# Later conditioning on TensorE behind the first tiles, query and key splits after their transposes, folded weights in plain float32

## The chip, the cores and the metric

The kernel runs on one core of one Trainium2 chip. The metric is device time in microseconds (us) for one launch. Five engines work side by side: TensorE (PE; its weight loads, PEld, overlap with it), VectorE (DVE), ScalarE (ACT), GpSimd (POOL) and SyncE (SP), whose queue issues the DMAs.

## The reference, cut to what matters

One step of a two-layer backbone on 1024 latent and 256 context tokens with 1024 channels. Both layers are modulated by a conditioning vector: `c` for latent tokens, `c_ctx` for context tokens.

```python
def ada_mod(cvec, w, b):
    m = jax.nn.silu(cvec) @ w + b              # (1024) @ (1024, 3072): shift, scale, gate
    return jnp.split(m, 3, axis=-1)

# each layer: h = rms_norm(x, g) * (1 + scale) + shift;  x = x + gate * mixer(h)
# layer 0: two attention mixers (A global, B windowed +-128 with a sink logit), 8 query and
#   2 key/value heads of 64 each; A's q and k are RMS-normed per head; rotary positions on
#   latent q and k; latent tokens also attend to cached context keys and values;
#   y = concat(oa * silu(ga), ob * silu(gb)) @ w_out
# layer 1: u, gate = split(h @ w_in, 2);  y = (Re(fft2(u in 4 groups of 256)) * silu(gate)) @ w_out
# at the end: rms_norm(x, final_g)
```

Outputs are the two token streams and the new context keys and values of layer 0.

## The kernel before, in words

**Precision.** Most matmuls are split: each operand is held as a high part (float32r, a rounded float32) and a low part (the rest), and `mm3` (L236) adds three products, hi x hi, hi x lo and lo x hi. `split` (L259) makes the parts, one cast and one subtraction. A matmul on tiles of type float32 that were not split runs in plain float32; the first layer's conditioning does so already.

**Buffers.** `take(tag, ...)` gives a buffer of a zone (`u` 26, `w` 8, `q` 2, `pt` 3, `p` 4, `h` 9, `e` 4), the one that has been free longest among the zones named; `drop` gives it back. PSUM has eight banks in four tags; transposes go through the three banks of `t`.

**Order of the work.** The program is written out flat, and the framework's planner orders each engine's queue, SP's too, by a simulated timeline of its own with program order as priority. Attention and its fillers are ordered by hand: `attend` (L968) runs over units (128-query tile, group g, head pair pr; groups 0 and 1 are mixer A, 2 and 3 mixer B). A unit is `soft` (scores, row minima, exponential), then `weigh` of an earlier unit (transposes of the probabilities, split, product with the values), then `fl_.pump(budget)`, which lets queued filler work run up to a budget in us.

The stages:

1. *Start.* Group 0's folded weights (`fold_load` L506, `fold_piece` L526: layer 1's input weights times the channel Fourier matrix, written to DRAM as `wcd`, `wsd`), the loads of x, and for each of 8 channel chunks the layer-0 shift and scale on TensorE (`ada_load` L468, `ada_chunk` L477: two tiles of 8 x 128 x 128 weights, 16 plain matmuls of the 2-column conditioning with 128 columns of weights, then two small transposes), modulation, and the first key and query products of tiles 0 to 3.
2. *First tiles* (`S1`, L31, loop at L799): norm and modulation of the other token groups, then keys and values (`kv_pair` L673) and queries (`q_pair` L723) of mixer A. Each of these evacuates a product, norms and rotates it, splits it (`split_v` L627, hi in 64 columns and lo in the next 64), and leaves a `post` for later: transposes of the split halves (`transp` L631, 128 columns a head) and their copy out of PSUM. Keys stay in SBUF for mixer A or go to DRAM (`kd`) for B; queries go to DRAM (`qd`) and are loaded by `load_q` (L830) when a unit needs them. `fl_.depth` posts are held back.
3. *Attention A and B*, with fillers in the order of `ORDER` (L50): query weights, mixer B's keys, folded weights f1, gates g0 to g3, folded weights f2, f3. In qb0, qb1 and g0 stands the later conditioning, `COND` (L51): the gate of layer 0 and the shift and scale of layer 1. `cond_steps` (L1017) calls `Rows.step_ap` (L340) for each of 8 rows of weights (4 KB a partition): two products added up on VectorE for the latent vector (L345), a scaled copy on ScalarE (L349) and an addition on GpSimd (L350) for the context vector. `Rows.finish` (L369) splits the accumulators and sums them over partitions with 8 matmuls of 512 columns (L359), then writes the gate to DRAM (`gtd`) or transposes shift and scale into columns (`row_to_mod` L300).
4. *Turn to the output projection.* `weigh` stores each unit's output to DRAM (`od`, through `store` L929) at once; when all units of a row tile are finished, `proj_load` and `proj_step` (L1207, L1216) load it back with gates and softmax totals and multiply by `w_out` (tile name `oz`). Output weights come through `out_weights` (L983).
5. *Layer 1*: gates (`g1E`, `g1O`, `g1c`), Fourier products (`u`, `pc`, `ps`), output projection (`of`).

Of the kernel before, what the change touches and what calls it, by code (L numbers as in the profile page):

```python
# [9 lines left out]
F32 = mybir.dt.float32  # L10
# [7 lines left out]
P = 128  # L18
D = 1024
NT = 10  # L20
# [13 lines left out]
EF = 1  # L34
PLACE = (
# [9 lines left out]
FC, XF = 1.3, False  # L45
AT_C, WO1 = (1, 1), ((0, 1, 2, 3), (), (4,), (5, 6), (7,))
# [4 lines left out]
COND = ("qb0", "qb1", "g0")  # L51
# [70 lines left out]
def hybrid_step(ctx: ExitStack, tc: tile.TileContext, I, O):  # L122
# [44 lines left out]
    qd = dr.tile([NT, 4, 2, 64, 512], F32, name="qd")  # L167
# [26 lines left out]
    bT1 = cp.tile([P, 8], F32, name="bT1")  # L194
# [121 lines left out]
    class Rows:  # L316
# [23 lines left out]
        def step_ap(self, k):  # L340
            wt = take(self.tags, (P, D))
            sp.dma_start(wt.a, ada_src(self.l, self.part, k))
            for h in range(2):
                sl = slice(h * 512, h * 512 + 512)
                dve.scalar_tensor_tensor(  # L345
                    out=self.acc[0][:, sl], in0=wt[:, sl], scalar=cs[:, k, 0:1], in1=self.acc[0][:, sl],
                    op0=ALU.mult, op1=ALU.add,
                )
            act.activation(wt.a, wt.a, AF.Copy, scale=cs[:, k, 1:2])  # L349
            pool.tensor_add(self.acc[1].a, self.acc[1].a, wt.a)  # L350
            drop(wt)

# [114 lines left out]

    def ada_load(k):  # L468
        out = []
        for part in range(2):  # L470
            raw = take(("p", "pt", "q"), (P, 8, P))
            c0 = part * D + k * P
            sp.dma_start(raw.a, I["ada_w"][0, :, c0 : c0 + P].rearrange("(b p) c -> p b c", p=P))
            out.append(raw)
        return out

    def ada_chunk(k, raws):  # L477
        ps = bank("g", f"ada{k}")
        for part, raw in enumerate(raws):
            for b in range(8):  # L480
                pe.matmul(
                    ps[0:2, part * P : part * P + P], cs[:, b, :], raw[:, b, :], start=b == 0, stop=b == 7
                )
            drop(raw)
# [7 lines left out]
        dve.tensor_scalar(moda[:, 0, k, :], tp[:, 2:4], bT1[:, k : k + 1], gT[:, 0, k : k + 1], op0=ALU.add, op1=ALU.mult)  # L492
# [13 lines left out]
    def fold_load(g):  # L506
        if "f" not in fold:
            fraw = take("h", (P, 2, 256))
            sp.dma_start(fraw.a, I["fch"])
            fold["f"] = (take("h", (P, 2, 256), F32R), take("h", (P, 2, 256), F32R))  # L510
            split(fold["f"][0].a, fold["f"][1].a, fraw.a)
            drop(fraw)
        wu = []
        for j in range(2):
            hi = take("w", (P, 1024), F32R)
            lo = take("w", (P, 1024), F32R)
            for hf in range(2):
                raw = take("h", (P, 512))
                sl = slice(hf * 512, hf * 512 + 512)
                sp.dma_start(raw.a, I["wuT"][(2 * g + j) * P : (2 * g + j + 1) * P, sl])  # L520
                split(hi[:, sl], lo[:, sl], raw.a, XE["wh"], E_WL)
                drop(raw)
            wu.append((hi, lo))
        return wu

    def fold_piece(g, kb2, wu, tag="g", later=None):  # L526
        fh, fl = fold["f"]
        acc = bank(tag, f"wa{g}{kb2}")
        for i in range(2):
            c0 = (2 * kb2 + i) * P  # L530
            mm3(
                acc[:, i * 256 : i * 256 + 256],
                [(wu[j][0][:, c0 : c0 + P], wu[j][1][:, c0 : c0 + P], fh[:, j, :], fl[:, j, :]) for j in range(2)],
            )
# [13 lines left out]
        if kb2 == 3:  # L548
            for h, l in wu:
                drop(h, l)  # L550
            fold["n"] = fold.get("n", 0) + 1
            if fold["n"] in (EF, 4):
                drop(fh, fl)
# [14 lines left out]
    dve.tensor_scalar(bT1, bT[:, 0, 8:16], 1.0, None, op0=ALU.add)  # L568
# [62 lines left out]
    def transp(name, y2, n):  # L631
        tp = t_bank(name, F32R)
# [1184 lines left out]
```

## Time and profile before

| | |
|---|---|
| median of 3 runs | 1280.24 us (1274.92 to 1284.47) |
| profiled execution, its own time | 1273.2 us |
| its span | 1271.3 us |
| DMA moved in all | 168.28 MB, 132 GB/s on average |
| mean granted TensorE clock | 0.979 |

In the profile `out<-in` names the tiles an instruction writes and reads, with buffer numbers left out (`h`, `w`, `u` and so on are the zones). Matmuls and weight loads are both listed with their line; a line can be that of a helper such as L243 in `mm3`. Durations of single matmuls include the pipeline's depth, so that a row of n matmuls takes less than n times the mean. The chain of waits follows the work that ended last back from the end: at each step to what released it.

### The profile page before, as it was taken

To read this page: it belongs to the slowest core of one execution; us is meant where nothing else is said; L and a number is where in the kernel's file an instruction comes from. 1 tells how busy PE (TensorE), PEld (TensorE's weight loads), DVE (VectorE), ACT (ScalarE), POOL (GpSimd) and SP (SyncE) were. 2 spreads that over 40 slices of the span, in tenths; PEclk is the share of its full clock that TensorE was granted. 3 is DMA by queue.
4 is the path that set the end of the run, shared out by engine and by line. 5 is a ranking of instruction groups with operands and counts; after the bars stand their busy time and mean duration, and the time that the engine had idled before them with its cause. 6 is when DMAs were issued, how large, how long until landed. Compare 5 with 4: busy or idle time off the path is not lost.

```text
span 1271.3 us, 21928 instructions
## 1 busy us (share of the span) xinstructions
PE 1194.0 (94%) x7867; PEld 1061.1 (83%) x7867; DVE 928.8 (73%) x2105; ACT 625.9 (49%) x1223; POOL 458.7 (36%) x376
## 2 busy tenths in 40 slices
PE   7979999999899899999999979789999998999997
PEld 6769999999789888888999978667777888988886
DVE  4478888776987987868887868466775888558553
ACT  4343466665575576755756676431264324333121
POOL 4256665423785764530101042310411216335001
PEclk9989999999999999999999989889999999999999
DMA  9902322324634345444332398597412544345321
GB/s 306 291 5 66 92 91 57 115 72 120 179 101 137 96 139 176 120 129 128 90 107 80 93 264 205 154 254 199 134 42 76 163 152 142 101 156 177 132 85 66
DMA packets 156198, 168.28 MB, mean 132 GB/s; under 512 B 21917, under 2 KB 117161, under 8 KB 156090
## 3 DMA queue, kind: packets, MB, share of 16 engines
q1 hardware_dynamic: 156090, 166.89, 44.6%
q8 instruction: 62, 1.02, 0.4%
q14 instruction: 46, 0.38, 0.1%
HBM read 122.67 MB, written 44.18 MB: 131 GB/s over the span
## 4 chain that ended last, share of the span: by engine, by line
PE 69%; DVE 12%; DMA 9%; issue 4%; POOL 3%; ACT 2%; SPq 1%; POOLq 0%; DVEq 0%; ACTq 0%
PE of L243 9%; PE ga L243 8%; PE av L951 7%; PE pt L945 6%; PE oz L243 5%; PE q L243 4%; PE u L243 4%; PE g1E L243 4%; PE g1O L243 3%; PE sL L828 3%; PE kv L243 2%; DVE w L345 2%; PE sC L828 2%; PE g1c L243 2%; DVE p L862 2%
## 5 line engine op out<-in xcount | busy, mean ns | idle before, releaser
L948 DVE TENSOR_TENSOR pt<-pt,pt 128x512 fp32r<-128x512 f32 (+1 forms) x264 | 170.9, 657 | 32.2 <-ACT pt L255 31.9
L951 PE MATMUL av<-pt,u 128*128 128x256 f32 x1008 | 171.3, 292 | 7.8 <-DVE pt L948 4.5
L255 ACT ACTIVATE pt<-pt 128x512 fp32r<-128x512 f32 (+1 forms) x264 | 146.9, 574 | 60.9 <-PE pt L945 35.6
L945 PE MATMUL pt<-identr,p 128*128 128x128 f32 x1008 | 156.6, 274 | 0.8 <-ACT h L255 0.5
L951 PEld LDWEIGHTS av<-pt,u 128*128 128x128 f32 x1008 | 142.1, 192 | 17.1 <-DVE pt L948 7.8
L261 POOL TENSOR_TENSOR w<-h,w 128x512 fp32r<-128x512 f32 x58 | 76.8, 1337 | 184.6 <-ACT w L255 79.0
L243 PE MATMUL q<-w,u 128*128 128x256 f32 x864 | 130.4, 291 | 0.7 <-ACT h L731 0.7
L945 PEld LDWEIGHTS pt<-identr,p 128*128 128x128 f32 x1008 | 119.6, 141 | 9.9 <-DVE pt L948 1.0
L243 PE MATMUL ga<-u,w 128*128 128x512 f32 (+1 forms) x576 | 123.6, 360 | 0.1
L869 ACT ACTIVATE p<-p,nm 128x1280 f32<-128x1280 f32 (+1 forms) x80 | 95.4, 1192 | 54.5 <-DVE p L862 54.0
L243 PEld LDWEIGHTS q<-w,u 128*128 128x128 f32 x864 | 115.7, 193 | 4.3 <-ACT h L731 1.2
L243 PEld LDWEIGHTS ga<-u,w 128*128 128x128 f32 x576 | 93.8, 188 | 15.0 <-ACT pt L255 0.6
L828 PE MATMUL sL<-u,q 128*128 128x512 f32 x256 | 85.0, 417 | 10.4 <-DVE p L862 8.3
L243 PE MATMUL oz<-u,w 128*128 128x512 f32 x240 | 69.2, 416 | 11.2 <-ACT w L255 11.2
L869 ACT ACTIVATE p<-p,NM 128x640 f32<-128x640 f32 (+2 forms) x80 | 59.2, 740 | 32.8 <-DVE p L862 32.7
L350 POOL TENSOR_TENSOR w<-w,w 128x1024 f32<-128x1024 f32 x24 | 58.4, 2433 | 44.6 <-ACT w L349 33.7
L828 PE MATMUL sC<-u,q 128*128 128x256 f32 x320 | 63.4, 301 | 9.0 <-DMA q<-qd 5.2
L243 PE MATMUL of<-u,u 128*128 128x512 f32 (+1 forms) x219 | 66.0, 389 | 0.0
L243 PEld LDWEIGHTS oz<-u,w 128*128 128x128 f32 x240 | 46.6, 200 | 21.6 <-ACT w L255 11.9
L828 PEld LDWEIGHTS sC<-u,q 128*128 128x128 f32 x320 | 49.1, 193 | 13.1 <-DMA q<-qd 5.8
L862 DVE TENSOR_SCALAR_CACHE_REDUCE p<-sC,nsink 128x256 f32<-128x256 f32 x80 | 37.8, 475 | 30.2 <-PE sC L828 25.2
L345 DVE SCALAR_TENSOR_TENSOR w<-w,cs,w 128x512 f32<-128x512 f32 x48 | 52.7, 1136 | 5.3 <-DMA w<-i_ada_w 4.2
(771 smaller groups left out, 2802.8 us busy)
## 6 DMA issues: line engine op xcount, KB each, us to landing
q<-qd SPq DMA_DIRECT2D x80, 256.0 KB
w<-i_ada_w SPq DMA_DIRECT2D x24, 512.0 KB
h<-i_w_in SPq DMA_DIRECT2D x40, 256.0 KB
qd<-h SPq DMA_DIRECT2D x40, 256.0 KB
h<-i_w_out SPq DMA_DIRECT2D x32, 256.0 KB
h<-i_wuT SPq DMA_DIRECT2D x16, 256.0 KB
u<-i_x SPq DMA_DIRECT2D x8, 512.0 KB
p<-i_ada_w SPq DMA_DIRECT2D x8, 512.0 KB
```

The costliest lines, as they stand in the source:

```text
L243: pe.matmul(out, a, b, start=i == 0, stop=i == n - 1)
L255: act.activation(out, in_, AF.Copy)
L261: pick("lo" + lc, lc).tensor_sub(dst_l, src, dst_h)
L345: dve.scalar_tensor_tensor(out=self.acc[0][:, sl], in0=wt[:, sl], scalar=cs[:, k, 0:1], in1=self.acc[0][:, sl], op0=ALU.mult, op1=ALU.add,)
L350: pool.tensor_add(self.acc[1].a, self.acc[1].a, wt.a)
L828: pe.matmul(ps, q[:, s, hc * P : hc * P + P], keys, start=s == 0, stop=s == 1)
L862: dve.tensor_scalar(p[i][:, end[i] : end[i] + n], ps, sign, last[i], op0=ALU.mult, op1=ALU.min, accum_out=c)
L869: act.activation(p[i][:, 0 : end[i]], p[i][:, 0 : end[i]], AF.Exp, bias=last[i], scale=-1.0, accum_out=SU[:, t, hd + i, 0:1],)
L945: pe.transpose(tp[:, jj * 256 + i * P : jj * 256 + i * P + P], p[i][:, off : off + P], ident)
L948: dve.tensor_sub(pt[:, 1, 0:n], tp[:, 0:n], pt[:, 0, 0:n])
L951: pe.matmul(acc, vv, pt[:, s, jj * 256 : jj * 256 + 256], start=c + jj + s == 0, stop=c + jj == nt - 1 and s == 1,)
```

## The change

- *Later conditioning.* `step_ap`, `cond_steps` and `COND` go. Instead 24 column tiles (gate of layer 0, shift and scale of layer 1, 8 each) are loaded as the first layer's are (512 bytes a row), multiplied on TensorE by the 2-column conditioning (8 plain float32 matmuls each) and placed between the steps of the first tiles: `AT_N` says how many before each step. A gate tile gets its bias and goes to DRAM; a shift or scale tile is copied out, transposed (one tile later) and modulated.
- *Splits after transposes.* `kv_pair` and `q_pair` transpose the unsplit float32 result, two heads in 128 columns, so half as many transposes, and make hi and lo out of PSUM: one copy and one subtraction (`key_split`, `post`). `qd` and `kd` have another layout; `load_q`, `scores` and `swap_kv` follow it. Cached keys are treated the same way, with both heads' columns loaded.
- *Folded weights.* `fold_load` keeps the weights and the Fourier matrix unsplit, `fold_piece` multiplies them in plain float32.
- *Order.* In the first tiles two posts are held back, not one. `attend` loads the next unit group's queries after the current one's second head pair. `weigh` leaves its stores in `held`, which are issued after the next unit's `soft` or ahead of a projection's loads. Group 2's key and value buffers are dropped after its last unit, no longer after all of attention.

```diff
+QPRE, HOLD = 1, 0
+QE_Z = ("pt", "q", "w", "u", "p")
-COND = ("qb0", "qb1", "g0")
+AT_N, AT_Z = (0, 0, 3, 0, 3, 2, 2, 2, 2, 2, 3, 3, 3), ("p", "pt", "q")
+AT_P = ((0, 2), (1, 0), (1, 1))
...
-        def step_ap(self, k):
...
+    def ada_tile(l, part, k, tags):
+        raw = take(tags, (P, 8, P))
+        c0 = part * D + k * P
+        sp.dma_start(raw.a, I["ada_w"][l, :, c0 : c0 + P].rearrange("(b p) c -> p b c", p=P))
+        return raw
+
+    def ada_mm(out, raw):
+        for b in range(8):
+            pe.matmul(out, cs[:, b, :], raw[:, b, :], start=b == 0, stop=b == 7)
+        drop(raw)
...
     def fold_load(g):
         if "f" not in fold:
-            fraw = take("h", (P, 2, 256))
...
+            fold["f"] = take("h", (P, 2, 256))
+            sp.dma_start(fold["f"].a, I["fch"])
         wu = []
         for j in range(2):
-            hi = take("w", (P, 1024), F32R)
-            lo = take("w", (P, 1024), F32R)
...
+            wu.append(take("w", (P, 1024)))
+            sp.dma_start(wu[j].a, I["wuT"][(2 * g + j) * P : (2 * g + j + 1) * P, :])
...
-            mm3(
...
+            for j in range(2):
+                pe.matmul(
+                    acc[:, i * 256 : i * 256 + 256], wu[j][:, c0 : c0 + P], f[:, j, :], start=j == 0, stop=j == 1
+                )
...
+    def key_split(dst, tp, h):
+        a, b = 64 * h, 64 - 64 * h
+        copy("kev", E_KEV, dst[a : a + 64], tp[a : a + 64])
+        dve.tensor_sub(dst[b : b + 64], tp[a : a + 64], dst[a : a + 64])
...
-        y2 = []
-        for i in range(2):
-            y2.append(take(HZ[0], (P, 4, P), F32R))
-            split_v(y2[i].a, y[:, i])
...
         def post():
+            tp = transp(f"qT{m}{kv}{t}", y.rearrange("p t (a h) d -> p (t a) (h d)", h=2), 4)
+            tv = tp.rearrange("p (t n) -> p t n", t=2)
+            qe = take(QE_Z, (P, 2, 2, 256), F32R)
+            copy("qev", E_QEV, qe[:, :, 0, :], tv)
+            dve.tensor_sub(qe[:, :, 1, :], tv, qe[:, :, 0, :])
             for i in range(2):
-                tp = transp(f"qT{m}{kv}{t}{i}", y2[i].a, 4)
-                qe = take("h", (P, 512))
-                copy("qev", E_QEV, qe.a, tp)
-                sp.dma_start(qd[t + i, 2 * m + kv].rearrange("a d f -> (a d) f"), qe.a)
-                drop(qe, y2[i])
+                sp.dma_start(qd[t + i, 2 * m + kv], qe[:, i].rearrange("p a n -> p (a n)").bitcast(F32))
+            drop(qe, qb)
...
-    fl_.depth = 1
+    fl_.depth = 2
...
+    def ada_turn():
+        l, part, k, row = turn_later.popleft()
+        tp = t_bank(f"mt{l}{part}{k}")
+        pe.transpose(tp[:, 0:2], row[:, 0, :], ident[0:2, 0:2])
...
+    def ada_fill(n):
+        for _ in range(min(n, len(todo_ada))):
+            l, part, k = todo_ada.popleft()
+            raw = ada_tile(l, part, k, AT_Z)
...
+            ps = t_bank(f"ad{l}{part}{k}")
+            ada_mm(ps[0:2, 0:P], raw)
+            if part == 2:
+                dve.tensor_add(row[:, 0, :], ps[0:2, 0:P], row[:, 1, :])
+                sp.dma_start(gtd[l, :, sl], row[:, 0, :])
+                drop(row)
+            else:
+                act.activation(row[:, 0, :], ps[0:2, 0:P], AF.Copy)
+                turn_later.append((l, part, k, row))
...
     for n, op in enumerate(S1):
         t = int(op[1])
+        ada_fill(AT_N[n])
...
+        held.append(put)
...
+            if (t, g) not in qs:
                 fl_.need(("q", t // 2 * 2, g))
                 qs[(t, g)] = load_q(t, g)
             pend.append((un, soft(t, g, pr, qs[(t, g)])))
             if pr == 1:
                 drop(qs.pop((t, g)))
+            nx = next((u[:2] for u in units[n:] if u[:2] != (t, g)), None)
+            if pr == QPRE and nx is not None and nx not in qs and ("q", nx[0] // 2 * 2, nx[1]) in fl_.done:
+                qs[nx] = load_q(*nx)
+            flush_held(HOLD)
...
-        if nm in cond:
-            for n in range(4):
-                cost, fn, key = (*work[n], None)[:3]
-                fl_.add(0.5 * cost, fn, key)
-                fl_.add(0.0, cond_steps(cond[nm], (2 * n,)))
-                fl_.add(0.5 * cost, cond_steps(cond[nm], (2 * n + 1,)))
...
+        if un == last_g2:
+            drop(*kvb[2])
...
         if gate is not None:
+            flush_held()
             ol = take(OB[0], (P, 8, P))
```

More of the change, by code (lines that the diff above doesn't have):

```diff
@@ L338, in step @@
                 drop(wt)
-        def step_ap(self, k):
[L341 to L351, printed above, removed]
         def half(self, h, ps, start=True, stop=True):
@@ L470, in ada_load @@
         for part in range(2):
[L471 to L474, printed above, removed]
+            out.append(ada_tile(0, part, k, ("p", "pt", "q")))
         return out
@@ L479, in ada_chunk @@
         for part, raw in enumerate(raws):
[L480 to L484, printed above, removed]
+            ada_mm(ps[0:2, part * P : part * P + P], raw)
         row = take("e", (2, 256))
@@ L507, in fold_load @@
         if "f" not in fold:
-            fraw = take("h", (P, 2, 256))
[L509 to L512, printed above, removed]
+            fold["f"] = take("h", (P, 2, 256))
+            sp.dma_start(fold["f"].a, I["fch"])
         wu = []
         for j in range(2):
-            hi = take("w", (P, 1024), F32R)
-            lo = take("w", (P, 1024), F32R)
[L517 to L523, printed above, removed]
+            wu.append(take("w", (P, 1024)))
+            sp.dma_start(wu[j].a, I["wuT"][(2 * g + j) * P : (2 * g + j + 1) * P, :])
         return wu
     def fold_piece(g, kb2, wu, tag="g", later=None):
-        fh, fl = fold["f"]
+        f = fold["f"]
         acc = bank(tag, f"wa{g}{kb2}")
@@ L824, in small, with q_at @@
         return sm.tile([P, n], F32, tag=tag, name=name, bufs=6)
+    def q_at(q, s, hc):
+        c0 = s * 256 + hc // 2 * P
+        return q[:, hc % 2, c0 : c0 + P]
     def scores(ps, q, hc, keys):
         for s in range(2):
-            pe.matmul(ps, q[:, s, hc * P : hc * P + P], keys, start=s == 0, stop=s == 1)
+            pe.matmul(ps, q_at(q, s, hc), keys, start=s == 0, stop=s == 1)
     def load_q(t, g):
@@ L961, in weigh, with put, flush_held @@
         dst = od[2 * g + pr].rearrange("(h d) n -> d h n", d=64)
-        store(dst, os_, t, lambda out: dve.tensor_add(out, a3[0:64], lo_sb.a))
-        drop(lo_sb, os_)
+        rev = t in (2, 3, 6, 7, 9)
+        dve.tensor_add(os_[..., ::-1] if rev else os_.a, a3[0:64], lo_sb.a)
+        drop(lo_sb)
+        def put():
+            for c0, b0, n in PLACE[t]:
+                sp.dma_start(dst[..., c0 : c0 + n], os_[..., b0 : b0 + n])
+            drop(os_)
+        held.append(put)
     pend = []
     qs = {}
+    held = deque()
+    def flush_held(n=0):
+        while len(held) > n:
+            held.popleft()()
     def attend(units, budget, lag, after):
@@ L997, in hybrid_step @@
     base = {"qa": C_QA, "qb": C_QB, "kb": C_KB, "g": C_G}
-    cond = dict(zip(COND, ((0, 2), (1, 0), (1, 1))))
-    rows, wout = {}, []
+    wout = []
     ws["qa0"] = wqa0
@@ L1013, in fn @@
             drop_w(ws[nm])
-            return 0
-        return fn
-    def cond_steps(key, ks):
-        def fn():
-            if key not in rows:
-                rows[key] = Rows(*key, f"ad{key[0]}{key[1]}", "w")
-            for k in ks:
-                rows[key].step_ap(k)
-            if ks[-1] == 7:
-                rows[key].finish("g")
             return 0
@@ L1081, in swap_kv @@
             fl_.need(("kb", t))
-        sp.dma_start(K[g].bitcast(F32), kd[h, :, 0:1024])
-        sp.dma_start(KC[g][:, 256:512].bitcast(F32), kd[h, :, 1024:1280])
+        for i in range(2):
+            rows, part = slice(64 * h, 64 * h + 64), slice(64 * (i ^ h), 64 * (i ^ h) + 64)
+            sp.dma_start(K[g][part].bitcast(F32), kd[i, rows, 0:1024])
+            sp.dma_start(KC[g][part, 256:512].bitcast(F32), kd[i, rows, 1024:1280])
         sp.dma_start(V[g].bitcast(F32), vd[h, 0:8].rearrange("t p d -> p t d"))
@@ L1314, in hybrid_step @@
         after(u0)
-    for b in kvb[2] + kvb[3]:
+    for b in kvb[3]:
         drop(b)
```

93 lines of the change are left out of this document (56 added, 37 removed).

## The prediction

> **What bounds the kernel now.** I read the page's busy shares first, then busy time by stage, the chain of waits, the costliest groups and the waits of TensorE.
>
> ```profile
> span 1271.3 us, 21928 instructions
> ...
> PE 1194.0 (94%) x7867; PEld 1061.1 (83%) x7867; DVE 928.8 (73%) x2105; ACT 625.9 (49%) x1223; POOL 458.7 (36%) x376
> ```
>
> TensorE (PE) is busy for 94% of the span, so work added to it is paid in time unless it lands in a gap. The stages say where gaps are. Columns: length, busy us (instructions) of PE, PEld, DVE, ACT, POOL; granted clock; DMA share; GB/s.
>
> ```profile
> 0.00:75.00 75.00, 66.23 (x531) 55.59 (x531) 32.66 (x73) 27.76 (x50) 24.89 (x27) 1.00 0.85 255
> 75.00:140.00 65.00, 53.13 (x394) 49.78 (x392) 56.62 (x126) 23.39 (x48) 46.04 (x43) 0.87 0.21 62
> 140.00:300.00 160.00, 160.00 (x1277) 153.35 (x1276) 126.30 (x322) 100.16 (x169) 74.57 (x79) 1.00 0.27 77
> 300.00:550.00 250.00, 231.70 (x1699) 209.55 (x1699) 215.12 (x449) 159.81 (x267) 151.12 (x107) 1.00 0.48 142
> 550.00:725.00 175.00, 174.97 (x1171) 160.13 (x1170) 136.36 (x430) 105.54 (x246) 16.24 (x14) 1.00 0.36 100
> 725.00:875.00 150.00, 125.99 (x714) 109.04 (x713) 99.02 (x244) 77.33 (x176) 40.30 (x23) 0.91 0.77 207
> ```
>
> 140:300 and 550:725 are full: there only PE's own work counts. PE is idle for 8.8 us in 0:75, 11.9 in 75:140 (the first tiles of layer 0), 18.3 in 300:550 (attention with the later conditioning as filler) and 24.0 in 725:875 (attention turning into the output projection). More is hidden. In 75:140 the clock is 0.87, so 13% of 53.1 us, 7 us, is work at a lower clock: 19 us lost in all. In 725:875 the same step gives 0.09 x 126 = 11, so 35. In 300:550 the visible 18.3 is a lower bound; at the 125 ns per record of 140:300 (160.00 us / 1277) its 1699 records need 213 us, so 37 is an upper one. The stage has a few more 512-wide matmuls than 140:300, so I take the middle, 27.
>
> The Trainium skill ("Perfetto Trace Analysis", Identifying the Most-Contended Engine) says to judge TensorE's headroom by weight-load busy time, not matmul busy time. By that rule 300:550 at the 96% of 140:300 would need 209.55 / 0.958 = 219 us, a loss of 31, and the sum below would come out 4 us lower.
>
> **The work on PE, part by part.** Chain of waits (start, length, what):
>
> ```profile
> 43.82 3.58 PE ada L481 x32
> 269.98 1.31 PE pt L945 x12
> 310.33 1.42 DVE w L345 x2
> 388.38 4.72 DMA w<-i_ada_w
> 474.80 1.42 PE wa L243 x12
> 745.32 6.82 DMA q<-qd
> 764.94 7.60 DMA od<-e
> 860.37 16.02 PE oz L243 x68
> ```
>
> *Later conditioning.* The first layer's chunk (L481) is the same operation as the added one: 16 plain float32 matmuls, 32 records, 112 ns apart. So a plain matmul is two records and one tile (8 matmuls) 1.79 us; 24 tiles add 43.0 us. Both operands' shapes are those of the row, so there is no doubt on this term. Removed are 24 matmuls of 512 columns that fold the accumulators (8 for each of three vectors), at 16.02 / 68 = 236 ns: -5.7. The small transposes into modulation columns are 16 before and after.
>
> *Folded weights.* A piece now takes 12 split matmuls in 1.42 us (118 ns each). After, it takes 4 plain ones of 256 columns: 8 records. No row shows a plain matmul that wide. Below: 8 x 118 ns = 0.94; above: 8 x 236 (the 512-wide row) = 1.89. Two records at twice the 128-wide 112 ns make 1.79, which I take since the chunk row is the same mode: +0.37 x 16 pieces = +5.9 (bounds -7.6 and +7.6).
>
> The Trainium skill ("FP8 and Floating Point Precision", TensorE Precision Notes) says true float32 takes four passes through the array, which speaks against this part: four in place of three would be 1.42 x 4/3 = 1.89 us a piece, an estimate, and the term +7.6. No row of before settles it at this width.
>
> *Transposes after the change.* 200 split transposes (160 query, 40 key) become 100 plain ones.
>
> ```profile
> L634 PE MATMUL qT<-identr,h 128*128 128x128 f32 x148 | 17.7, 239 | 0.5 <-POOL h L629 0.5
> L257 DVE CAST h<-h 128x256 fp32r<-128x256 f32 x47 | 21.2, 483 | 6.9 <-POOL h L659 2.6 <-ACT h L731 2.4 <-ACT h L679 1.7
> L629 POOL TENSOR_TENSOR h<-h,h 128x256 fp32r<-128x256 f32 x46 | 35.4, 784 | 18.0 <-DVE h L257 16.2 <-PE kT L634 0.7 <-ACT p L869 0.6
> L257 DVE COPY h<-qT 128x512 f32<-128x512 f32 x20 | 13.7, 683 | 2.9 <-PE qT L634 2.9
> L350 POOL TENSOR_TENSOR w<-w,w 128x1024 f32<-128x1024 f32 x24 | 58.4, 2433 | 44.6 <-ACT w L349 33.7 <-issue 8.9 <-DMA w<-i_ada_w 1.9
> L345 DVE SCALAR_TENSOR_TENSOR w<-w,cs,w 128x512 f32<-128x512 f32 x48 | 52.7, 1136 | 5.3 <-DMA w<-i_ada_w 4.2 <-DMA w<-i_ada_b 1.0
> L349 ACT ACTIVATE w<-w,cs 128x1024 f32<-128x1024 f32 x24 | 27.6, 1151 | 34.0 <-DVE w L345 17.1 <-issue 8.0 <-POOL h L629 4.6
> L261 POOL TENSOR_TENSOR w<-h,w 128x512 fp32r<-128x512 f32 x58 | 76.8, 1337 | 184.6 <-ACT w L255 79.0 <-PE ga L243 64.4 <-DVE w L257 36.0
> L333 DVE SCALAR_TENSOR_TENSOR u<-u,cs,u 128x512 f32<-128x512 f32 x20 | 16.4, 866 | 6.6 <-DMA u<-i_ada_w 6.6
> ```
>
> New ones cost 109 ns each (1.31 / 12, plain float32), 10.9 us. Old ones cost at most 17.7 / 148 = 120 ns, 24 us, and at least half of a new one: between -13 and 0; I take -6.
>
> PE's work thus grows by 43.0 - 5.7 + 5.9 - 6 = **+37 us** (bounds +17 to +45).
>
> **What PE's gaps give back.**
>
> ```profile
> PE oz L243 <- ACT w L255: 11.2, 3, 4.5
> PE sL L828 <- DVE p L862: 8.3, 8, 1.6
> PE wa L243 <- DVE w L257: 7.0, 2, 5.2
> ...
> PE sC L828 <- DMA q<-qd: 5.2, 1, 5.2
> ```
>
> *300:550, -24.* All of L345, L349 and L350 leave this stage: 52.7 us of DVE, 27.6 of ACT, 58.4 of POOL. DVE falls from 215 to about 162 of 250 us, below the 79% (126.3 / 160) at which 140:300 shows no PE gap. L345 takes 1136 ns where L333, the same operation at the kernel's end without a POOL partner at its side, takes 866: its cost was contention too. Chain entries such as "DVE w L345 x2" and the 4.72 us conditioning load go. Of the 27 us I leave 3 (bounds 0 to 12): what is late next is the softmax chain, the 8.3 us of PE on L862.
>
> *75:140, -15.* The added matmuls stand between the norm, key and query steps, and they depend on their own tile alone. DMA, at 0.21 here, has room: 24 tiles of 0.5 MB are 12.6 MB, 49 us at the 255 GB/s of 0:75. They queue on SP with 8 bias rows and 8 stores; behind them on that queue stand only the loads of the second query weights. The stage's DVE (56.6 of 65 us) sees almost no change: three query pairs save 2 x 483 ns of casts and one or two subtractions each and add a 682-ns-like subtraction out of PSUM, and 24 tiles add a small addition or scaling each. So 19 us of gap meets 43 us of independent matmul; I leave 4 (bounds 2 to 19). What the gap doesn't take, 28 us, lengthens the stage: attention starts at about 160 us, not at the 134 of this row (timeline of PE: start, length).
>
> ```profile
> 99.64 0.72 PE L243 MATMUL kv<-w,u 128*128 128x256 f32 x4
> 100.20 0.53 PE L243 MATMUL q<-w,u 128*128 128x256 f32 x3
> 100.56 3.13 PE L243 MATMUL kv<-w,u 128*128 128x256 f32 x25
> ...
> 134.00 0.73 PE L828 MATMUL sL<-u,q 128*128 128x512 f32 x2 [1.47 <-DMA q<-qd]
> ```
>
> *725:875, -12.* Loading queries one unit ahead covers the 5.2 us wait on q. If that cover is missing, the 6.82 us load of the chain is paid as now. The unsplit folds f2 and f3 take 8 x 1337 ns = 10.7 us off POOL just where the output weights are split, so projection matmuls can start earlier and fill gaps; of the 11.2 us of PE oz waits I count 7. Against it, an attention output's store now waits until the next unit's scores are planned: behind it on SP stand the projection's loads, and its buffer, one of four, waits with it (today the store of 7.60 us is on the chain). Bounds -24 to +4.
>
> *0:75, -2.* The first fold waits 7.0 us for its split, but DMA at 0.85 sets this stage's end; bounds -7 to 0.
>
> The rest (layer 1, key layout, cache loads, keys split out of PSUM, deeper post queue, an earlier release of three buffers) is taken at zero: stages 140:300 and 550:725 hide it under full PE, and uncovered the key and cache parts would cost some ten 0.5-us operations.
>
> Sum: +37 - 24 - 15 - 12 - 2 = **-16 us** on the profiled execution's 1273.2, 1257. That execution lies 0.55% under the median of the runs, 1280.24, so the median would be 1257 x 1.0055 = **1264 us**. With single terms off by their likely half the case reaches from 1253 to 1276.
>
> **Rivals.**
>
> *Serial first tiles (slower).* DVE is 87% busy in 75:140, and if the added matmuls sit in front of transposes that its chain needs (both use the same three PSUM banks), PE and DVE take turns: the 43 us are paid in full, the gap stays, and the stage adds some 5 us of small DVE operations. With nothing gained in 725:875: +37 - 24 - 2 + 5 = +16, 1296 us. It decides if attention's first scores come later than 134 + 43 = 177 us. For it: the waits on POOL and DVE are latency, not throughput. Against it: the planner already alternates matmuls of different accumulations at a grain of three or four (the rows at 100 us), so a tile need not stand whole in front of anything. Chance 0.13.
>
> *Work merely moved (no change).* The gap in 75:140 is filled by half (-8) and 725:875 gains only the q wait (-5): +37 - 24 - 8 - 5 - 2 = -2, 1278 us. This is also the case in which preloading and held stores alter nothing, because the planner had ordered the queue so already. Chance 0.19.
>
> *The turn to the projection closes too (faster).* With POOL and buffers free, 725:875 loses its 24 visible us, the conditioning stage all 27 and the first fold 5: +37 - 27 - 15 - 24 - 5 = -34, 1246 us. For it: 35 us are lost there, more than anywhere. Against it: 764.94 and other stores to DRAM and back are no shorter. Chance 0.18.
>
> **Numbers.** The forecast has 0.50. About 1% (12.8 us) can be told from no change. The forecast lies two thirds below 1267: 0.33 faster, 0.17 same. Faster: 0.33 + 0.18 = 0.51. Same: 0.17 + 0.19 = 0.36. Slower: 0.13. The range 1242 to 1290 takes in the faster rival and no change and leaves out most of the slower one; the forecast's own is 1253 to 1276.
>
> **What would show it.** The added tiles about 1.8 us each on PE between 70 and 160 us at a clock near 1.00 there; attention's first scores at about 160; no more than some 3 us of PE idle between attention's start and the turn; fold pieces near 1.8 us; no wait of sC on q near the turn; POOL's busy time down by some 100 us. The forecast is wrong if the tiles leave gaps in the first stage, or if PE idle after attention is 24 us as now.

## The result and the profile after

The changed kernel takes 1270.48 us (median of 13 runs, 1267.79 to 1279.9) against 1280.24 for the kernel before in the same comparison (13 runs). The ratio over all runs is 0.9942, with a 95% interval of 0.9918 to 0.9965; the two medians lie further apart than that. Two later comparisons of the same pair gave 0.9968 (0.9944 to 0.9992) and 0.9972 (0.9941 to 1.0003). So the change gains some 0.3 to 0.6%, 4 to 7 us, and the last interval just takes in no gain. The forecast was 1264 us, 16 us below.

The profiled execution's own time is 1269.79 us, 3.4 below that of before. From the page after, the span and the busy times:

```profile
span 1268.0 us, 22014 instructions
...
PE 1218.0 (96%) x8063; PEld 1073.5 (85%) x8063; DVE 874.0 (69%) x2036; ACT 586.4 (46%) x1179; POOL 314.0 (25%) x269
```

GpSimd lost 145 us of work and VectorE 55, and TensorE gained 24 us of busy time. The same stages as in the prediction, with the same columns:

```profile
0.00:75.00 75.00, 67.36 (x505) 54.47 (x506) 29.55 (x65) 25.66 (x46) 15.56 (x19) 0.98 1.04 303
75.00:140.00 65.00, 59.55 (x465) 45.77 (x464) 37.14 (x94) 20.35 (x42) 27.78 (x26) 0.95 0.50 138
140.00:300.00 160.00, 157.25 (x1234) 145.75 (x1232) 121.39 (x289) 79.40 (x144) 67.50 (x63) 1.00 0.29 86
300.00:550.00 250.00, 248.21 (x1880) 235.83 (x1880) 178.39 (x437) 143.37 (x255) 52.29 (x50) 1.00 0.34 98
550.00:725.00 175.00, 174.90 (x1183) 160.50 (x1181) 138.41 (x434) 108.66 (x247) 11.94 (x10) 1.00 0.39 109
725.00:875.00 150.00, 133.11 (x736) 111.25 (x735) 107.88 (x266) 78.25 (x178) 34.07 (x18) 0.98 0.77 212
```

In 300:550 the 18.3 us of visible TensorE idle shrank to 1.8, and in 725:875 the 24.0 shrank to 16.9. But 75:140 still idles 5.5 us at a clock of 0.95, and 140:300, which was full, now idles 2.8.

Busy time mixes work with slow work, so I also split TensorE's time record by record. Each record is charged the spacing that its kind has when it runs back to back: 109 ns for 128 columns, 118 for 256, 232 for 512, and 216 for the plain float32 records of 256 columns; the split transposes of the kernel before stand 59 to 87 ns apart and are charged some 85. That is its work. What is left of the time until the next record starts is slack: idle time, records at a lower clock, and turns from one kind of work to another. Worked out from the traces (us, until the last TensorE record, each figure rounded by itself):

```
                     before   after   change   predicted
work                   1139    1175    +36.2      +37
slack    0:75          15.8    15.4     -0.4       -2
slack   75:168         20.8    16.3     -4.5  } first tiles -15
slack  168:300          1.1     5.1     +4.0  }
slack  300:550         28.6     2.9    -25.7      -24
slack  550:725          1.4     0.7     -0.7        0
slack  725:875         38.9    25.2    -13.7      -12
slack  875 on          19.0    20.4     +1.4        0
sum                                     -3.2      -16
```

(First tiles end at attention's first scores, which started at 134.00 us before and start at 167.51 after; 168 is taken for both.) All the missing time is in one term.

The chain of waits shows why the first tiles did not fill (start, length, what):

```profile
75.31 3.37 PE ad L466 x30
...
82.44 1.63 PE ad L466 x14
...
86.78 1.34 DVE pt L654
...
88.77 0.77 DVE pt L655
89.54 1.41 DVE u L418
90.95 0.33 DVE q L639
91.28 1.47 DVE q L645 x2
92.75 0.73 DVE h L421
93.53 0.69 PE ckt L617 x2
94.22 7.52 PE ad L466 x48
```

`ad` are the added conditioning tiles, 16 records each. They run up to 84 us; then VectorE is on the chain with the norm and rotation of the first keys (L654 to L645, with a cast of the modulation, L418, between them), and only behind them, at 92.75, with the evacuation of a transposed chunk (L421). That frees a PSUM bank, and TensorE goes on. The 48 records that follow take 157 ns each, not the 112 of the first layer's: the clock had dropped in the gap. Windows before and after the drop (columns as above):

```profile
88.40:91.80 3.40, 1.13 (x9) 0.86 (x8) 3.40 (x5) 2.23 (x3) 3.04 (x3) 1.00 0.00 0
91.80:98.65 6.85, 5.12 (x24) 3.02 (x25) 4.20 (x8) 0.86 (x2) 6.37 (x6) 0.50 0.26 77
```

The waits of TensorE have the same place as a row, with the others that matter:

```profile
PE wa L516 <- DMA w<-i_wuT: 5.8, 1, 5.8
...
PE oz L246 <- ACT q L258: 4.2, 1, 4.2
...
PE ckt L617 <- DVE h L421: 3.5, 1, 3.5
...
PE sC L864 <- DMA q<-qd: 0.2, 1, 0.2
```

The longest row of `oz` on ACT went from 11.2 us to 4.2 (all rows of `oz` together from 14.3 to 9.5), the 5.2 us of `sC` on queries to 0.2.

### The profile page after: what moved, and what is told of

It reads as the page before. It is cut to its first block, busy times and chain, and to the rows that moved or that the text cites. A ratio compares the mean times of both kernels' runs of the same rounds, so it can differ in the third digit from the quotient of the medians.

```text
span 1268.0 us, 22014 instructions
## 1 busy us (share of the span) xinstructions
PE 1218.0 (96%) x8063; PEld 1073.5 (85%) x8063; DVE 874.0 (69%) x2036; ACT 586.4 (46%) x1179; POOL 314.0 (25%) x269
## 4 chain that ended last, share of the span: by engine, by line
PE 83%; DMA 7%; DVE 4%; ACT 2%; issue 1%; POOL 1%; SPq 1%; POOLq 0%; DVEq 0%; ACTq 0%
PE ga L246 9%; PE of L246 9%; PE av L987 8%; PE pt L981 7%; PE q L246 7%; PE oz L246 6%; PE sL L864 4%; PE u L246 4%; PE kv L246 4%; PE ad L466 4%; PE g1E L246 4%; PE g1O L246 3%; PE sC L864 3%; PE ada L466 2%; PE g1c L246 2%; PE wa L516 2%
## 5 line engine op out<-in xcount | busy, mean ns | idle before, releaser
L987 PE MATMUL av<-pt,u 128*128 128x256 f32 x1008 | 168.7, 290 | 2.3 <-DVE e L999 1.5
L264 POOL TENSOR_TENSOR w<-h,w 128x512 fp32r<-128x512 f32 x42 | 55.5, 1338 | 133.3 <-DVE w L260 96.7
L864 PE MATMUL sL<-u,q 128*128 128x512 f32 x256 | 81.0, 410 | 3.9 <-DMA q<-qd 2.3
L905 ACT ACTIVATE p<-p,NM 128x640 f32<-128x640 f32 (+2 forms) x80 | 59.1, 740 | 25.2 <-DVE p L898 25.0
L264 POOL TENSOR_TENSOR u<-h,u 128x512 fp32r<-128x512 f32 x19 | 25.8, 1363 | 171.4 <-ACT u L258 160.3
L246 PE MATMUL oz<-u,u 128*128 128x512 f32 x240 | 63.0, 397 | 3.4 <-DVE h L1180 1.6
L639 POOL TENSOR_TENSOR h<-h,rope 128x512 f32<-128x512 f32 (+1 forms) x18 | 21.7, 1206 | 148.7 <-ACT h L722 99.5
L246 PE MATMUL kv<-w,u 128*128 128x256 f32 x384 | 57.9, 289 | 0.0
L246 PEld LDWEIGHTS oz<-u,u 128*128 128x128 f32 x240 | 44.5, 188 | 14.6 <-issue 2.0
L898 DVE TENSOR_SCALAR_CACHE_REDUCE p<-sL 128x512 f32<-128x512 f32 x64 | 43.8, 684 | 18.4 <-PE sL L864 9.3
L898 DVE TENSOR_SCALAR_CACHE_REDUCE p<-sL,nm 128x512 f32<-128x512 f32 x64 | 47.6, 744 | 7.8 <-PE sL L864 6.5
```

Source lines behind the costliest of these rows:

```text
L246: pe.matmul(out, a, b, start=i == 0, stop=i == n - 1)
L264: pick("lo" + lc, lc).tensor_sub(dst_l, src, dst_h)
L639: pick("rope", XE["rope"]).tensor_mul(t1.rearrange("p t h (b c) -> p t (h b) c", b=2), y.rearrange("p t h (b c) -> p t (h b) c", b=2), cb)
L864: pe.matmul(ps, q_at(q, s, hc), keys, start=s == 0, stop=s == 1)
L898: dve.tensor_scalar(p[i][:, end[i] : end[i] + n], ps, sign, last[i], op0=ALU.mult, op1=ALU.min, accum_out=c)
L905: act.activation(p[i][:, 0 : end[i]], p[i][:, 0 : end[i]], AF.Exp, bias=last[i], scale=-1.0, accum_out=SU[:, t, hd + i, 0:1],)
```

## The experiments

### Each half alone, and neither

Four kernels: the later conditioning left out of either kernel, and each half of the change without the other.

```diff
 after_no_later, before_no_later: no later conditioning
+    dve.memset(modb[:, 1], 0.0)
+    dve.memset(moda[:, 1], 1.0)      # and constants to gtd
 later_only: before, with ada_tile, ada_fill, AT_N of the change and COND = ()
 rest_only:  after, with step_ap, cond_steps, COND of before and AT_P = ()
```

> The changed kernel without any later conditioning: the 24 tiles, their matmuls, small transposes and loads are left out, and constants stand in their place (gate 0.5, scale 1, shift 0), so its time is that of the rest. Prediction's theory: a gap of 15 us in the first tiles takes part of the 43 us of matmuls, so leaving them out saves 28 us: 1242 us, ratio to before 0.971. Rival (what the trace after suggests): almost nothing was taken by the gap, so leaving them out saves 41 to 44 us: 1228 us, ratio 0.960, and attention's first scores come back from 167 to about 130 us.

> The kernel before without any later conditioning (left out, constants in its place). Prediction's theory: it cost 24 us of lost PE time in 300:550 and 6 us of 512-wide matmuls, 30 us in all: 1250 us, ratio 0.977. Rival: only the visible idle of that stage came from it, some 12 of 18 us, and the rest is attention's own: 1262 us, ratio 0.986.

> The kernel before with the conditioning part of the change alone. Prediction's theory: +43 - 6 - 24 - 15 = -2 us, 1278 us, ratio 0.999. Rival (the first gap takes nothing): +43 +1 - 7 - 26 = +11 us, 1291 us, ratio 1.009, so this part alone loses and all of the gain is from the other parts.

> The changed kernel with the conditioning back on VectorE, ScalarE and GpSimd in attention. Prediction's theory: +6 (fold) - 6 (transposes) - 12 (turn) - 2 (start) = -14 us, 1266 us, ratio 0.989. Rival (this part carries the whole gain, since the conditioning part loses 11): -21 us, 1259 us, ratio 0.984.

Measured, as ratios to the kernel before: without the conditioning 0.9674 (0.9623 to 0.9726) after and 0.9829 (0.9773 to 0.9884) before; the conditioning part alone 1.016 (1.01 to 1.0219); the rest alone 1.0105 (1.0047 to 1.0162). On the kernel before's 1275.43 us of that comparison these are 1235.61, 1254.4, 1296.32 and 1291.94 us.

So each half alone makes the kernel slower, and together they make it faster. Both halves came out slower than either of their two cases. later_only's trace has 42 us more work than that of before and only 18 us less slack. The conditioning on TensorE costs some 34 to 38 us beside the other edits (0.9942 or 0.9968 against 0.9674). Its full work is 42 us by the two traces, so the gaps took some 4 to 8 us of it, between the 15 of the theory and the nothing of the rival. On the other engines it cost 21 us in the kernel before (1275 - 1254) and 56 beside the other edits (1292 - 1236). The second figure was not foreseen.

### Why the old conditioning was dear beside the other edits

The change lets the query steps take their output buffers from five zones (`QE_Z`), among them `w`, in which the old conditioning keeps its accumulators and weight rows.

```diff
 rest_no_w: rest_only with
-QE_Z = ("pt", "q", "w", "u", "p")
+QE_Z = ("pt", "q", "u", "p")
```

> rest_only (the changed kernel with the old conditioning on VectorE, ScalarE and GpSimd), but the query post steps may not take buffers of zone w, which the old conditioning's accumulators and weight rows use; everything is computed. If the shared w buffers made the old conditioning dear there (56 us against 21 in the kernel before), the idle time of 300 to 575 us falls from 49 towards 29 us and the time by 15 to 25 us, to about 1270. If it is contention of the engines' operations (or the half-length preparation of queries in front of it), it stays within 5 us of rest_only's 1.0105.

1270.52 us, 0.9949 (0.9924 to 0.9974); by the ratios 20 us below rest_only, as the first case had it. Slack in 300:550 fell from 40.6 to 31.5, in 550:725 from 6.8 to 1.4 and in 725 to 875 from 32.7 to 27.8. Waits of the old conditioning's VectorE step on its weights between 300 and 600 us (in all, times, longest), in rest_only:

```profile
DVE w L349 <- DMA w<-i_ada_w: 25.8, 11, 10.2
```

in rest_no_w:

```profile
DVE w L349 <- DMA w<-i_ada_w: 13.2, 9, 4.0
```

and in the kernel before:

```profile
DVE w L345 <- DMA w<-i_ada_w: 4.2, 4, 1.5
```

The sharing made the weight loads late; without it they still wait longer than in the kernel before. And the changed kernel with the conditioning left where it was, but without that sharing, is as fast as the changed kernel: 0.9949 against 0.9942 to 0.9972. Moving the conditioning to TensorE bought nothing that these runs can tell; it traded 32 us of slack (118.0 against 86.1) for 36 us of work.

### The first tiles

First the gap at 89.7 us. One kernel moves what waits there, the transposes of the cached keys (`c0`), to a later step; `AT_N` changes with it, so that each other step keeps its tiles:

```diff
 cache_later
-S1 = "c1 n2 m1 c0 m2 K0 Q0 Q2 K2 k6 q8 k4 k8"
+S1 = "c1 n2 m1 m2 K0 Q0 Q2 K2 c0 k6 q8 k4 k8"
-AT_N, AT_Z = (0, 0, 3, 0, 3, 2, 2, 2, 2, 2, 3, 3, 3), ("p", "pt", "q")
+AT_N, AT_Z = (0, 0, 3, 3, 2, 2, 2, 2, 0, 2, 3, 3, 3), ("p", "pt", "q")
 after_again: the changed kernel beside it
```

> The changed kernel itself, beside the next three on the same chip: 1270 us, ratio to before 0.994, as measured.

> The changed kernel with the cached keys of head 0 prepared after the third tile pair's queries, not between the two modulations. Theory: the added tiles can't fill the gap of the first tiles because PE takes its queue in order, and tiles stand behind a transpose of cached keys that waits 3.7 us for VectorE, after which the clock is at half for 3 us. Then the gap of 90 to 94 us goes and 4 to 7 us are saved: 1265 us, ratio 0.990. Rival: the wait is VectorE's own chain, another transpose takes its place at the head of the queue, and nothing changes: 1270 us.

after_again 0.9968, cache_later 0.9994 (0.9967 to 1.002): no gain. The wait is still there, with the next conditioning tile in the place of the cached keys. In cache_later's timeline (start, length, engine, what, and the idle time before it):

```profile
92.67 0.80 DVE L421 TENSOR_SCALAR h<-xt,moda,modb 128x512 f32<-128x512 f32 x1
...
93.52 3.57 PE L466 MATMUL ad<-p,cs 128*2 128x128 f32 x16 [3.52 <-DVE h L421]
```

A tile that reads nothing of `xt` waits for the instruction that evacuates `xt`. What they share is the banks of `t`. So the tiles of the first ten steps got another bank, `g`, which no other instruction uses there; own_low also moves the first six of them behind the two modulation steps in program order:

```diff
 own_bank
-    def ada_fill(n):
+    def ada_fill(n, own=False):
...
-            ps = t_bank(f"ad{l}{part}{k}")
+            ps = bank("g" if own else "t", f"ad{l}{part}{k}")
...
-        ada_fill(AT_N[n])
+        ada_fill(AT_N[n], n <= 9)
 own_low, besides
-AT_N = (0, 0, 3, 0, 3, 2, 2, 2, 2, 2, 3, 3, 3)
+AT_N = (0, 0, 0, 0, 0, 5, 3, 3, 3, 2, 3, 3, 2)
```

(In `n <= 9`, `n` is the step's number, counted from 0.)

> The changed kernel, but the conditioning tiles placed before the ninth step of the first tiles accumulate in the single PSUM bank g, which is free until then, in place of a bank of t; everything is computed. In the changed kernel TensorE idles from 89.72 to 93.5 us because the third t bank is held by a transposed chunk whose evacuation on VectorE stands behind four microseconds of the key chain. Theory (the gap refuses the tiles because they need the same three banks as the transposes): with a bank of their own the idle 3.7 us and most of the 2.5 us of waits between transposes are filled, attention's first scores come at about 162 us instead of 167.5, and the time falls by 4 to 7 us, to about 1265. Rival (VectorE's chain sets the stage, the bank is only where it shows): the gap reappears at another instruction, first scores stay within 2 us of 167.5, the time within 3 us of the changed kernel's.

> As own_bank, and the six tiles placed ahead of the two modulation steps come after them in program order, so that the planner gives them a lower priority than the transposes and products there; everything is computed. Theory of the banks: with a free bank the planner may still pull them forward into the gaps, so the same 4 to 7 us below the changed kernel, perhaps 2 more since no tile stands ahead of a transpose. Rival: the time within 3 us of the changed kernel's, with the slack of 75 to 168 us at 16 us as before.

> The changed kernel once more, as the measure for the runs beside it: about 0.995 of the kernel before.

> The changed kernel with the first tiles' conditioning in bank g, again, on the same chip as after_five. The 4 us of slack that left 75 to 168 us and the 1.2 us of 168 to 300 should be in the total if nothing later gives them back: 3 to 6 us below after_five. Rival: the stages behind wait for something that does not depend on when attention starts, and the total is within 2 us of after_five.

In own_bank tiles run where the gap was, and the stage keeps its full clock. Its windows:

```profile
75.00:140.00 65.00, 60.89 (x499) 47.10 (x498) 36.97 (x99) 21.10 (x44) 28.46 (x26) 1.00 0.55 156
```

and its timeline:

```profile
90.97 1.91 PE L466 MATMUL ad<-pt,cs 128*2 128x128 f32 x16
...
160.83 0.62 PE L864 MATMUL sL<-u,q 128*128 128x512 f32 x2
```

First scores come 6.7 us earlier, but with one tile still to follow; the second pair of scores, at 170.52 for 175.00, comes 4.5 us earlier. Slack of 75:168 falls from 16.3 to 12.4. So the bank was the cause of the gap. Of the total only a little is seen: 0.994 (0.991 to 0.997) and 0.9945 (0.991 to 0.998), against 0.9972 for after_five beside the second; about 3 us, with intervals that overlap. own_low, 0.9971 (0.994 to 1.0002), gained nothing: its slack there is 17.1.

What is left in 75:168 was sorted by what stands on each side of it (worked out from the traces, us):

```
                                        after   own_bank   burst   burst_two
waits over 0.3 us                         6.2        5.4     7.1         4.6
turns to and from 2-column work           4.8        4.9     3.8         3.0
the rest (lower clock, small)             5.3        2.1     1.7         1.8
```

A turn can be read in the timeline after:

```profile
146.95 1.30 PE L246 MATMUL kv<-w,u 128*128 128x256 f32 x9
148.19 1.91 PE L466 MATMUL ad<-q,cs 128*2 128x128 f32 x16
150.03 0.22 PE L799 MATMUL mt<-identr,e 2*128 2x2 f32 x1
150.18 1.22 PE L246 MATMUL kv<-w,u 128*128 128x256 f32 x8
```

The last of the nine products starts at 147.98; 118 ns later the tile could start, and it starts at 148.19, 0.09 us late. Sixteen records at 109 ns end at 149.93, and the small transpose starts at 150.03, again 0.09 us late. Each change between 128-column work, the tiles with their 2-column stationary operand and the small transposes costs some 0.06 to 0.09 us, and there are 55 of them (56 in own_bank). `burst` collects four tiles' rows in one wide row and runs four small transposes in a row; `burst_two` also gives the tiles bank `g` only for even `k`, and `t` otherwise.

```diff
 burst: own_bank, and
-        pe.transpose(tp[:, 0:2], row[:, 0, :], ident[0:2, 0:2])
+        for i in range(4):
+            pe.transpose(tp[:, 2 * i : 2 * i + 2], row[0:2, i * P : i * P + P], ident[0:2, 0:2])
 burst_two: burst, and
-            ps = bank("g" if own else "t", ...)
+            ps = bank("g" if own and k % 2 == 0 else "t", ...)
```

> own_bank, and the small transposes that turn shift and scale into columns run four at a time from one wide row instead of one after each tile; everything is computed. Theory (turns between 2-column tiles and 128-column work cost about 0.09 us each, 60 of them 6.3 us): some 24 to 30 turns go, first scores come 2 to 2.5 us earlier than in own_bank, the time falls by as much, and the remaining turns still cost about 0.09 us each. Rival (the 0.09 us is overlap with something else that then shows elsewhere): the slack of the first tiles stays at 12 us.

> burst, but the tiles alternate between bank g and the three banks of t; everything is computed. Theory: the two waits of tile on tile (2.2 us) that appeared in burst go while its 16 saved turns stay saved, so the first tiles' slack falls from 12.6 to about 10 us and the time to 2 us below burst. Rival: a tile in a bank of t waits for the transposed chunks again, and slack and time stay where they were.

burst lost 12 turns and 1.1 us of them, at the 0.09 us each that were expected (though the count of 60 and 6.3 us in its expectation took four waits for turns). It got waits in their place: its slack stays at 12.6 and its time, 0.9942 (0.9922 to 0.9962), at that of own_bank_five, as its rival has it. The longest of the waits on a tile, and the row of own_bank beside it:

```profile
PE ad L466 <- DVE e L824: 1.6, 1, 1.6
...
PE ad L466 <- ACT e L822: 1.1, 5, 0.3
```

Both are a tile waiting for the evacuation of the one before it, in the single bank. burst_two, with both kinds of banks, has fewer turns still (35 against 56 in own_bank) and shorter waits than burst: slack of 75:168 is 9.5, and the time 1263.68 us, 0.9895 (0.987 to 0.9919). Apart from the two without the later conditioning it is the fastest of this study, some 6 to 10 us below the changed kernel by the ratios, where 2 us below burst were expected and 6 came. The profile shows 3.1 us of that against burst in this stage; the later stages differ by up to 6 us both ways between the two traces and nearly cancel, so where the other microseconds are from stays open.

Last, another way to compute the 16 shift and scale tiles: weights stationary, the two conditioning columns moving, so that no small transposes are needed.

```diff
 columns
-            ada_mm(ps[0:2, 0:P], raw)
+            for b8 in range(8):
+                pe.matmul(tp[:, 0:2], raw[:, b8, :], cs[:, b8, :], start=b8 == 0, stop=b8 == 7)
```

> The changed kernel with the 16 shift and scale tiles multiplied the other way round: the weights (128 x 128) are the stationary operand and the two conditioning columns the moving one, so the result is already in columns, and the copy, the 16 small transposes and the turns between them go; the 8 gate tiles stay. Theory: a tile costs 1.79 us of matmuls and about 0.2 us more for each turn from the 2-column operand to 128-column work and back (203 and 209 ns against 109 and 118 in the trace), and again for its small transpose; without them 16 tiles save 0.3 to 0.5 us each, 5 to 8 us: 1264 us, ratio 0.989. Rival: a plain float32 weight load of 128 columns, twice for each matmul, is dearer than the 128 columns it replaces, and a tile gets slower: 1275 us or more.

1294.22 us, 1.0152 (1.0118 to 1.0186), where 1264 was expected. A line of its chain and its windows:

```profile
110.16 18.03 PE ad L814 x96
```

```profile
75.00:140.00 65.00, 58.76 (x368) 51.19 (x366) 33.05 (x84) 15.74 (x29) 25.23 (x22) 0.77 0.48 135
140.00:300.00 160.00, 156.25 (x1172) 150.32 (x1171) 112.08 (x271) 71.71 (x128) 67.11 (x61) 0.94 0.26 80
```

On this stretch of the chain a record takes 188 ns on average, and the granted clock of the stage is 0.77. Shorter windows tell the two apart:

```profile
109.50:112.90 3.40, 3.40 (x32) 3.10 (x30) 2.35 (x7) 0.00 (x0) 3.40 (x4) 1.00 0.88 240
112.90:140.20 27.30, 27.30 (x130) 27.30 (x130) 7.92 (x22) 0.76 (x2) 3.76 (x4) 0.50 0.51 149
```

At a clock of 1.00 the records stand 112 ns apart, about as far as with the operands the other way round (109); at 0.50 they stand 213 apart. So the rival's reason, that a tile is slower by itself, does not hold; the clock is lower. It falls to half after 2.8 us of these records, with TensorE busy throughout, and stays there for 27 us. Why it falls under them is not shown.

### The turn to the projection, and the folded weights

```diff
 fold_split: folded weights split and multiplied in three products, as before the change
 no_preload:
-            if pr == QPRE and nx is not None and ...
+            if False and ...
-        held.append(put)
+        put()
 no_hold: only the second of these
 keep_g2:
-        if un == last_g2:
-            drop(*kvb[2])
```

> The changed kernel with the folded weights split again as before. Prediction's theory: 6 us less of matmuls against 7 us lost in the turn to the projection, where GpSimd splits eight more pieces: 1271 us, no change. Rival: the splits cost nothing there, and it is 5 us faster: 1265 us; other rival: they also delay the start, and it is 10 us slower: 1280 us.

> The changed kernel, but queries are loaded when a unit needs them and attention outputs stored at once, as before the change; everything is computed. My prediction's term for the turn counted 5 us for the query wait covered: then the wait of sC on q of about 5 us comes back and the time rises by 5 to 7 us, to about 1277. Rival (the planner had ordered the queue so already, or the gain comes from the free VectorE and GpSimd): within 2 us of the changed kernel.

> The changed kernel, but group 2's key and value buffers are kept to the end of attention, as before the change; everything is computed. My prediction took this edit at zero: within 2 us of the changed kernel. Rival (these buffers decide when the output weights and the projection's loads can start, and so are the larger part of the 13.8 us that the turn gained): 4 to 10 us slower, with the stage from 725 to 875 losing TensorE time.

> The changed kernel, but attention outputs are stored at once; queries are still loaded one unit ahead; everything is computed. If the early query loads make the 10 us that were lost without both, this stays within 3 us of the changed kernel. If the held stores make them (stores that wait for VectorE block the loads behind them on SP's queue), it is 6 to 10 us slower than the changed kernel, like no_preload.

fold_split is 1.0041 (1.001 to 1.0073), 9 us above after_again on the same chip, although its TensorE work is 5 us less: its slack of 725 to 875 is 32.5 us against 25.2 to 29.6 in the three traces of the changed kernel. From 1025 to 1200 it is 19.4 against after_again's 12.5, but after_five, the same kernel as after_again, has 18.2 there, so that difference can't be put down to the folds. That leaves 3 to 7 us on the turn; where the rest of the 9 lies stays open. no_preload is 1.0047 (1.0016 to 1.0078), 10 us above keep_g2 on its chip. keep_g2 is 0.9971 (0.9941 to 1.0001), as fast as the changed kernel. no_hold is 1.0018 (1.0001 to 1.0034), 6 us above after_five, at the low end of the case in which the held stores make the difference. So preloading and held stores together are worth about 10 us, of which the held stores make some 6; the 4 left for preloading are only a difference between two chips. By the traces the held stores act in 300:550, where no_hold has 6.9 us of slack and after_five 2.3, and not on the turn (28.0 against 29.6). There no_preload has 35.6, and a wait of 5.2 us is back:

```profile
PE sC L864 <- DMA scd<-e: 5.2, 1, 5.2
...
757.38 0.58 SPq L869 DMA_DIRECT2D q<-qd  x1
```

The row names a store of softmax totals, which the scores do not read. They start at 764.88, 7.5 us after the query load in the second line was issued; that this load ended the wait is argued from that, not shown. The stage 725:875 has lost TensorE time and clock again:

```profile
725.00:875.00 150.00, 129.62 (x702) 110.37 (x701) 100.30 (x254) 76.73 (x177) 31.57 (x17) 0.91 0.72 195
```

## Why the prediction was right or wrong

**TensorE's work, +37: right.** It grew by 36.2 us. Three rows of the chain after, a tile and two stretches of a folded piece:

```profile
106.68 1.84 PE ad L466 x16
...
488.49 0.86 PE wa L516 x4
...
493.75 1.99 PE wa L516 x8
```

The tile takes the 1.8 us of the first layer's row. For the piece no row stood before: 4 of its 8 records take 0.86 us, so 1.72 a piece, and a piece that stands whole on the chain 1.99, though the next instruction starts 1.64 us after the piece does. At the 216 ns between its records a piece is 1.73 us, near the 1.79 that was taken. The 1.89 us estimated from the four passes of the Trainium skill ("FP8 and Floating Point Precision", TensorE Precision Notes) is 9% above that.

**300:550, -24: right.** -25.7, and later_only, with this part alone, also leaves only 5.7 us of slack there, 22.9 less than before; what the changed kernel gains beyond that may be the held stores', which were not counted here (no_hold has 6.9). The clock and the full stage are as foreseen. VectorE fell to 178 us, not to 162. The 28.6 us found by spacing are near the 27 that I took. The 31 by weight-load busy time, the measure of the Trainium skill ("Perfetto Trace Analysis", Identifying the Most-Contended Engine), lie on the other side of them; neither is clearly better. But the price is not a property of the conditioning alone: it was 21 us of time in the kernel before, 56 with a shared buffer zone, and some 35 beside the other edits without the sharing. What makes 35 out of 21 was not tried.

**725:875, -12: right, and in the main for its reasons.** -13.7. The prediction counted 5 us for the query wait, which went, and in no_preload a wait of that length is back; and 7 for the unsplit folds, where fold_split has 3 to 7 us more slack. Of the edits that it took at zero one was tried alone, the earlier release of buffers, and it was zero (keep_g2). That held stores count against the gain was wrong in sign: without them the kernel is slower (no_hold). The plain folds gained more than was predicted, 9 us of time in all; the forecast has +6 of work against 7 on the turn and 2 in 0:75.

**75:140, -15: wrong, and this is the step that failed.** It said that the added matmuls "depend on their own tile alone", that "19 us of gap meets 43 us of independent matmul", and left 4. What was left is 16.3, and 4.0 more appeared in 168:300. Three things stood in its place:

- The tiles were not independent: they share three PSUM banks with the transposes, and a bank is freed only when VectorE gets to it behind the key chain. own_bank removed this gap. The idle time had a second cost, the lower clock of the 48 records behind it: at 157 ns for 112 they took 2 us more. The clock fell at 91.8 us, 1.8 us after the last transpose had ended at 90.0 (3.5 us ahead of 93.53). The Trainium skill ("TensorE: Matmul & The Clock Gate", Part 1) has the clock go to half after an idle window of about 3.4 us. The trace does not bear that out here: half of that idle time was enough.
- The filler had a price in the stage: 55 turns of some 0.09 us, 4.8 us. It was counted at the speed that it has in a long row.
- Waits over 0.3 us did fall, from 13.8 us to 6.2. About half of the gap was filled, and the turns and new waits behind it took that back. What the 3.6 us of new waits in 168:300 hang on was not tried; they are waits of the scores on queries and on VectorE.

Of the 14.5 us that the term is short, own_bank gives back 5.1 of slack (3.9 in 75:168, 1.2 in 168:300), though only about 3 us of time, and the turns are 4.8; for the some 5 us that are left no run shows one cause.

First scores were forecast at 160 and came at 167.51; with a bank of their own at 160.83.

**The rivals.** "Serial first tiles" named the right mechanism, the three shared banks, at the wrong price: its 177 us was not reached, and the turn gained in full. "Work merely moved" has nearly the right sum (-2 against -3.4) by other terms. "The turn closes too" did not happen: 25.2 us of slack are left there.

**From the profile to the median.** The forecast took the profiled execution of before, 0.55% below its median, and carried that over. The changed kernel's lies 0.05% below its own. So the ratio says 7.4 us less where the two profiles differ by 3.4: the traces are of executions that lie differently in their own spread, and a difference of 4 us between two of them says little.

## What to carry to other kernels

A filler that reads nothing of the late work can still wait for it, here through a shared bank; ask of each operand and of the output what frees it, and which instruction stands in front of that one. Count the filler at the price that it has between other work, turns and clock included, not at that of a long row. And when two edits are judged one by one, look at the buffers that both take from: here each half alone was 13 to 20 us slower than the kernel before, and leaving one zone out of a list was worth as much as the whole move to TensorE.

## What the runs showed of the hardware that was not expected

A change between 128-column work, the tiles with a 2-column stationary operand and their small transposes costs some 0.06 to 0.09 us each way on TensorE (12 turns fewer in burst, 1.1 us less). A plain float32 record with 128 stationary and 2 moving columns takes 112 ns at a granted clock of 1.00, about as long as one with 2 stationary and 128 moving (109). Under a row of the former the clock fell to 0.50 with TensorE busy for 27.30 of 27.30 us, and the records then stood 213 ns apart: in columns busy time hid a halved clock. A plain float32 product of 256 columns takes two records of 216 ns, 432 ns against 3 x 118 = 354 for the split one, and the kernel still gained 9 us by it (fold_split), 3 to 7 of them on the turn, where GpSimd has eight pieces less to split.
